# A convolution over pairs of tiles with its taps on ScalarE, weight sums kept in HBM, and 18 of 44 down groups by seven products instead of 12

## The chip, the core and the metric

The kernel runs on one core of a Trainium2 chip. The metric is the time of one execution on the device in microseconds; lower is better. Before the change the median of three timed runs is 1498.99 us.

## What is computed

One transformer block on 256 tokens of width 2048, batch 1. A mixer (forgetting attention, stick-breaking attention, attention over 256 memory tokens, gated and summed, projected by `w_out`) is followed by a feed-forward part. The change concerns the feed-forward part only:

```python
h2 = rms_norm(x, g_ffn[l])
u = causal_depthwise_conv(h2 @ w_up[l], conv_w[l], conv_b[l])   # 3 taps per channel
u_gate, u_val = jnp.split(u, 2, axis=-1)                        # 5632 channels each
x = x + (jax.nn.silu(u_gate) * u_val) @ w_down[l]               # 5632 -> 2048
```

All inputs are float32, and the output is compared in float32 precision.

## The kernel before, in words

**Precision.** Every weight is split into two float32r parts: `hi`, a rounded copy made by ScalarE, and `lo`, the rest, made by VectorE as `raw - hi`. Activations are held as hi and lo halves side by side (256 + 256 columns). A product takes three matmuls (hi by hi, lo by hi, hi by lo), or, in the up stage, one matmul of 512 columns (`hi` weights against hi and lo activations at once, L739) and one of 256 columns (`lo` weights against hi activations, L740).

**Weights.** `piece` (up stage, L130 to L141) and `load` with `parts` (down stage, L783 to L794) bring 512 KB of weights per step. SyncE (SP) issues the DMA into one of four `raw` buffers, ScalarE casts it into one of four `hi` buffers (L136, L792), VectorE makes the `lo` (L137, L793). SP has one queue in program order, so a load whose buffer isn't free holds up the loads behind it. A `raw` buffer is free when `lo` is made, a `hi` or `lo` buffer when TensorE has used it.

**Up stage** (L729 to L745). Eleven steps `f0` over four channel tiles of 128; for each, `s = 0` (gate) and `s = 1` (value): 22 rounds. A round accumulates four tiles in four PSUM banks over eight pieces of two rows of tiles (`k`), 64 pairs of matmuls of L739 and L740. After the round each of the four tiles is handed to `conv` (L705), whose instructions are issued while the next round's matmuls run: ScalarE copies the lo half out of PSUM (L710), VectorE adds the hi half and multiplies by the row scale (L712, L713), ScalarE does the third tap with the bias (L716), VectorE the two others (L717, L718). In a value round follow the product with the gate (L724) and the split into `aT` (L169, L170).

**Down stage** (L865 to L894). The 44 channel tiles are 22 pairs, and the 2048 output columns are two halves `nb`: 44 groups of two tiles by 1024 columns, each a 2 by 2 by 2 block product. `eight` does a group as eight products of 128 by 512, 24 matmuls. `seven` does it as seven products (21 matmuls) in the Strassen-Winograd form: three products add straight into the outputs X, four go into extra sums Y, and `gather` (L846) adds up Y at the end of the half. The seven products need sums of the activations (`forms`, L767) and sums of the weights (t13 and t24, L828, L829, L832, L833), made by VectorE right in the group from the freshly loaded weights. The order of groups is a string: `plans = ("eeee" + "see" * 5 + "eee", "eee" + "se" * 7 + "eeeee")`, so 5 + 7 = 12 groups are done by seven products.

**What sets the order.** TensorE, ScalarE, VectorE, GpSimd and SP each run one queue in order; a scheduler places the instructions of each queue by priority when the program is built. `later` and `tick` say after which piece a `conv`, `gather` or the like is issued. A program's eight PSUM banks are handed out one at a time by `bank`.

## Time and profile before

| | |
|---|---|
| median of three timed runs (lowest to highest) | 1498.99 us (1498.02 to 1499.24) |
| span of the profiled execution, first to last instruction | 1494.4 us |
| TensorE / its weight loads busy | 99% / 84% of the span |
| VectorE / ScalarE / GpSimd busy | 68% / 53% / 1% |
| granted TensorE clock | full in every slice |
| DMA | 283.62 MB, mean 190 GB/s |
| up stage, first to last matmul | 766.0 to 1255.2 us |
| down stage, last matmul begins | 1489.7 us |

The page has no time of its own for the profiled execution beside its span; the median lies 4.6 us above the span, which is what lies around the first and the last instruction. In the rows of the profile, PE is TensorE, PEld its weight loads, DVE VectorE, ACT ScalarE, POOL GpSimd, and SP SyncE; `L137` is a line of the kernel. A row of a group gives the operation with its output and input, the count, then the time in all, the mean of one in ns, and the idle time ahead of it with what ended it.

### The profile page before, as it was taken

To read this page: it belongs to the slowest core of one execution; us is meant where nothing else is said; L and a number is where in the kernel's file an instruction comes from. 1 tells how busy PE (TensorE), PEld (TensorE's weight loads), DVE (VectorE), ACT (ScalarE), POOL (GpSimd) and SP (SyncE) were. 2 spreads that over 40 slices of the span, in tenths; PEclk is the share of its full clock that TensorE was granted. 3 is DMA by queue.
4 is the path that set the end of the run, shared out by engine and by line. 5 is a ranking of instruction groups with operands and counts; after the bars stand their busy time and mean duration, and the time that the engine had idled before them with its cause. 6 is when DMAs were issued, how large, how long until landed. Compare 5 with 4: busy or idle time off the path is not lost.

```text
span 1494.4 us, 19871 instructions
## 1 busy us (share of the span) xinstructions
PE 1483.2 (99%) x7429; PEld 1255.9 (84%) x7429; DVE 1014.0 (68%) x1465; ACT 794.0 (53%) x1108; POOL 16.1 (1%) x46
## 2 busy tenths in 40 slices
PE   8999999999999999999999999999999999999998
PEld 6888888888888888888888888888888888888777
DVE  5767566555655646555557778777778778987885
ACT  6755454358544444444456556556556656553552
POOL 0000000001000000000000000000000000000000
PEclk9999999999999999999999999999999999999999
DMA  8665475365666666655555665655656565556554
GB/s 291 193 211 158 126 220 167 119 211 164 188 194 210 185 210 203 185 190 190 184 182 183 198 191 184 196 190 184 198 187 191 186 196 183 199 188 228 185 202 140
DMA packets 138543, 283.62 MB, mean 190 GB/s; under 512 B 9275, under 2 KB 18127, under 8 KB 138447
## 3 DMA queue, kind: packets, MB, share of 16 engines
q1 hardware_dynamic: 137118, 280.26, 59.0%
q10 hardware_dynamic: 1328, 2.11, 0.4%
q8 instruction: 58, 0.95, 0.2%
q14 instruction: 39, 0.31, 0.1%
HBM read 280.23 MB, written 2.10 MB: 189 GB/s over the span
## 4 chain that ended last, share of the span: by engine, by line
PE 95%; DMA 2%; ACT 1%; DVE 1%; issue 0%; POOL 0%; SPq 0%; DVEq 0%; POOLq 0%; ACTq 0%
PE u L739 21%; PE u L740 11%; PE g L147 5%; PE g L148 5%; PE g L149 5%; PE x L797 4%; PE x L798 4%; PE x L799 4%; PE s L147 2%; PE s L149 2%; PE f L147 2%; PE f L149 2%; PE s L148 2%; PE f L148 2%; PE o L147 2%; PE o L149 2%
## 5 line engine op out<-in xcount | busy, mean ns | idle before, releaser
L739 PE MATMUL u<-hT,hi_u 128*128 128x512 f32 x1408 | 488.5, 392 | 0.0
L740 PE MATMUL u<-hT,lo_u 128*128 128x256 f32 x1408 | 395.1, 281 | 0.0
L739 PEld LDWEIGHTS u<-hT,hi_u 128*128 128x128 f32 x1408 | 263.3, 187 | 57.3
L137 DVE TENSOR_TENSOR lo_u<-raw_u,hi_u 128x1024 fp32r<-128x1024 f32 x176 | 215.4, 1224 | 116.0 <-ACT hi_u L136 115.9
L740 PEld LDWEIGHTS u<-hT,lo_u 128*128 128x128 f32 x1408 | 266.8, 189 | 0.0
L136 ACT CAST hi_u<-raw_u 128x1024 fp32r<-128x1024 f32 x176 | 184.7, 1050 | 138.4 <-PE u L739 106.5
L137 DVE TENSOR_TENSOR lo_g<-raw_g,hi_g 128x1024 fp32r<-128x1024 f32 x96 | 117.7, 1229 | 101.3 <-ACT hi_g L136 98.8
L136 ACT CAST hi_g<-raw_g 128x1024 fp32r<-128x1024 f32 x96 | 100.7, 1051 | 121.8 <-PE g L148 97.4
L147 PE MATMUL g<-hi_g,xT 128*128 128x512 f32 x384 | 151.1, 393 | 0.0
L149 PE MATMUL g<-lo_g,xT 128*128 128x512 f32 x384 | 149.8, 390 | 0.0
L148 PE MATMUL g<-hi_g,xT 128*128 128x512 f32 x384 | 149.7, 390 | 0.0
L792 ACT CAST hi_d<-raw_d 128x1024 fp32r<-128x1024 f32 (+1 forms) x88 | 86.7, 993 | 74.6 <-PE x L798 38.7
L793 DVE TENSOR_TENSOR lo_d<-raw_d,hi_d 128x1024 fp32r<-128x1024 f32 (+1 forms) x88 | 99.8, 1148 | 16.2 <-ACT hi_d L792 16.2
L797 PE MATMUL x<-hi_d,aT 128*128 128x512 f32 x268 | 104.4, 390 | 0.0
L799 PE MATMUL x<-lo_d,aT 128*128 128x512 f32 x268 | 104.4, 390 | 0.0
L798 PE MATMUL x<-hi_d,aT 128*128 128x512 f32 x268 | 104.4, 390 | 0.0
L149 PEld LDWEIGHTS g<-lo_g,xT 128*128 128x128 f32 x384 | 72.1, 188 | 15.2
L148 PEld LDWEIGHTS g<-hi_g,xT 128*128 128x128 f32 x384 | 72.2, 188 | 14.5
L147 PEld LDWEIGHTS g<-hi_g,xT 128*128 128x128 f32 x384 | 72.2, 188 | 14.6
L137 DVE TENSOR_TENSOR lo_s<-raw_s,hi_s 128x1024 fp32r<-128x1024 f32 (+1 forms) x40 | 44.7, 1118 | 37.2 <-ACT hi_s L136 37.2
L137 DVE TENSOR_TENSOR lo_f<-raw_f,hi_f 128x1024 fp32r<-128x1024 f32 (+1 forms) x40 | 44.7, 1120 | 34.5 <-ACT hi_f L136 33.0
L136 ACT CAST hi_f<-raw_f 128x1024 fp32r<-128x1024 f32 (+1 forms) x40 | 38.5, 966 | 52.5 <-PE f L148 47.6
(318 smaller groups left out, 2554.3 us busy)
## 6 DMA issues: line engine op xcount, KB each, us to landing
raw_u<-in_w_up_dram SPq DMA_DIRECT2D x176, 512.0 KB, 4.0
raw_g<-in_w_in_dram SPq DMA_DIRECT2D x96, 512.0 KB, 3.6
raw_d<-in_w_down_dram SPq DMA_DIRECT2D x88, 512.0 KB, 4.7
raw_f<-in_w_in_dram SPq DMA_DIRECT2D x32, 512.0 KB, 3.5
raw_s<-in_w_in_dram SPq DMA_DIRECT2D x32, 512.0 KB, 3.4
raw_o<-in_w_out_dram SPq DMA_DIRECT2D x32, 512.0 KB, 4.7
raw_kv<-in_w_mem_kv_dram SPq DMA_DIRECT2D x15, 512.0 KB, 5.4
raw_b<-in_w_br_fox_dram SPq DMA_DIRECT2D x12, 512.0 KB, 4.0
```

The lines of the kernel that those rows point to most:

```text
L136: pin(nc.scalar.copy(hi[:, :m], raw[:, :m]))
L137: pin(nc.vector.tensor_tensor(lo[:, :m], raw[:, :m], hi[:, :m].bitcast(F32), ALU.subtract))
L147: nc.tensor.matmul(o, lhsT=xh, rhs=wh, start=first, stop=False)
L148: nc.tensor.matmul(o, lhsT=xl, rhs=wh, start=False, stop=False)
L149: nc.tensor.matmul(o, lhsT=xh, rhs=wl, start=False, stop=last)
L739: nc.tensor.matmul(ps[i], lhsT=hi[:, j, c], rhs=hT[:, k + j, :], start=first, stop=False)
L740: nc.tensor.matmul(ps[i][:, :S], lhsT=lo[:, j, c], rhs=hT[:, k + j, :S], start=False, stop=last)
L792: nc.scalar.copy(hi[:, :n], src)
L793: nc.vector.tensor_tensor(lo[:, :n], src, hi[:, :n].bitcast(F32), ALU.subtract)
L797: nc.tensor.matmul(o, lhsT=ah, rhs=w[0], start=first, stop=False)
L798: nc.tensor.matmul(o, lhsT=al, rhs=w[0], start=False, stop=False)
L799: nc.tensor.matmul(o, lhsT=ah, rhs=w[1], start=False, stop=last)
```

## The change

**Convolution.** `conv` now takes a pair of tiles whose sums lie in two neighbouring PSUM banks, allocated together (`two_banks`, a pool of four pairs in place of eight single banks from the up stage on). Each instruction of 256 columns per tile becomes one of 512 per pair, except where a tap's factor differs by tile. The first and second taps, one fused multiply-add on VectorE each, become a multiplication on ScalarE (L738, one per tile and tap) into a scratch tile and an addition on VectorE (L739, one per pair and tap). The scaled sums `u` of all pairs share one buffer; there were two.

**Weight sums.** The four sums of a group's weights that `seven` needs are made in the up stage by `weight_sums`, one group in each of the first 18 rounds: SP loads the group's two weight tiles (2 x 512 KB) into `r`, VectorE makes the four sums in place, GpSimd's queue writes the 1 MB to a tensor T in HBM. In the down stage `seven` loads the sums (2 x 512 KB, `load_sums`) and the weights (256 KB + 512 KB, since one quarter isn't needed by itself), and VectorE only splits them.

**Plans.** `PLANS = ("eee" + "se" * 8 + "eee", "eee" + "se" * 4 + "sse" * 3 + "ee")`: 8 + 10 = 18 groups by seven products, so 26 by eight.

**Memory.** `aT` is split in two (36 and 8 tiles) so that `r` has room during the first 36; forms 8 and 9 go into the slots of tiles that are used up. The first up matmul waits for a pair of banks.

The diff, cut to its core:

```diff
+NSEVEN = (8, 10)
+PLANS = ("eee" + "se" * 8 + "eee", "eee" + "se" * 4 + "sse" * 3 + "ee")
...
     def bank(name):
+        if pp2:
+            return pp2[0].tile([P, 2, 512], F32, tag="pair", name=name)[:, 0]
         return pp.tile([P, 512], F32, tag="bank", name=name)
...
+    ppx.close()
+    pp2.append(ctx.enter_context(tc.tile_pool(name="pp2", bufs=4, space=bass.MemoryType.PSUM, reuse_waits="tile")))
...
+    def scratch(name):
+        return sm.tile([P, 512], F32, tag="junk", bufs=2, name=name).rearrange("p (i s) -> p i s", i=2)
+
+    def conv(ps, f, s):
+        taps_of = lambda j, i: taps[:, j, s * FT + f + i : s * FT + f + i + 1]
+        cr = scratch(f"cr_{f}_{s}")
+        nc.scalar.copy(cr, ps[:, :, S:])
+        nc.vector.tensor_tensor(cr, cr, ps[:, :, :S], ALU.add)
+        nc.vector.tensor_tensor(u[:, :, 2:], cr, rbc.unsqueeze(1).to_broadcast([P, 2, S]), ALU.mult)
+        y = cp.tile([P, 2, S], F32, tag="y", name=f"y_{f}_{s}")
         for i in range(2):
...
-        nc.scalar.activation(y, u[:, 2:], AF.Identity, scale=tap(2), bias=tap(3))
-        nc.vector.scalar_tensor_tensor(y, u[:, 1 : S + 1], tap(1), y, ALU.mult, ALU.add)
-        nc.vector.scalar_tensor_tensor(y, u[:, 0:S], tap(0), y, ALU.mult, ALU.add)
+            nc.scalar.activation(y[:, i], u[:, i, 2:], AF.Identity, scale=taps_of(2, i), bias=taps_of(3, i))
+        for j in (1, 0):
+            z = scratch(f"z{j}_{f}_{s}")
+            for i in range(2):
+                nc.scalar.activation(z[:, i], u[:, i, j : j + S], AF.Copy, scale=taps_of(j, i))
+            nc.vector.tensor_tensor(y, y, z, ALU.add)
...
+    def weight_sums(nb, p):
+        n0 = nb * PIECE
+        r = sp.tile([P, 2, 2, 512], F32, tag="r", name=f"r_{nb}_{p}")
+        for j in range(2):
+            tc.keep_in_program_order(
+                nc.sync.dma_start(r[:, j].rearrange("p a n -> p (a n)"), dv[:, 2 * p + j, n0 : n0 + PIECE])
+            )
+        yield
+        b01 = r[:, 0, 1]
+        tc.keep_in_program_order(nc.vector.tensor_tensor(r[:, 0, 0], r[:, 0, 0], b01, ALU.add))
+        tc.keep_in_program_order(nc.vector.tensor_tensor(b01, b01, r[:, 1, 1], ALU.add))
+        yield
+        tc.keep_in_program_order(nc.vector.tensor_tensor(r[:, 1, 1], r[:, 1, 1], r[:, 0, 0], ALU.add))
+        tc.keep_in_program_order(nc.vector.tensor_tensor(r[:, 1, 0], r[:, 1, 0], r[:, 1, 1], ALU.add))
+        T = dram.tile([P, 2, 1024], F32, name=f"T_{nb}_{p}")
+        nc.gpsimd.dma_start(T, r.rearrange("p a b n -> p a (b n)"))
+        made[nb, p] = T
+        yield
...
+                if k in (2, 8, 12):
+                    for a in adding:
+                        next(a)
                 tick()
-            for i in range(4):
-                later(conv(ps[i], f0 + i, s))
+            for i in (0, 2):
+                later(conv(pairs[i // 2], f0 + i, s))
...
+    def load_sums(T, h, name):
+        t = down_pool().tile([P, PIECE], F32, tag="tt", name=f"tt{h}_{name}")
+        nc.sync.dma_start(t, T[:, h])
+        return t
...
     def seven(p, n0, X, Y, first, last):
         k0, k1 = 2 * p, 2 * p + 1
-        raw0, raw1 = load(k0, n0), load(k1, n0)
-        t13 = sums(f"t13_{n0}_{p}")
-        t24 = sums(f"t24_{n0}_{p}")
-        b01, b11 = raw0[:, 512:], raw1[:, 512:]
-        nc.vector.tensor_tensor(t13[:, :512], raw0[:, :512], b01, ALU.add)
-        nc.vector.tensor_tensor(t13[:, 512:], b11, b01, ALU.add)
-        (B00,) = parts(raw0[:, :512], f"d{n0}_{k0}")
+        T = made[n0 // PIECE, p]
+        raw0, raw1 = load(k0, n0, 512), load(k1, n0)
+        t13, t42 = (load_sums(T, h, f"{n0}_{p}") for h in range(2))
+        (B00,) = parts(raw0, f"d{n0}_{k0}")
         three(Y[0], *a_of(k0, 0), B00, first, last)
-        nc.vector.tensor_tensor(t24[:, :512], t13[:, :512], b11, ALU.add)
-        nc.vector.tensor_tensor(t24[:, 512:], t24[:, :512], raw1[:, :512], ALU.add)
         B10, B11 = parts(raw1, f"d{n0}_{k1}")
...
-    plans = ("eeee" + "see" * 5 + "eee", "eee" + "se" * 7 + "eeeee")
```

Three places show how the change moves instructions in the queues of the engines. In the rows the number at a name's end is only a buffer's, `[waits ...]` names what the instruction waits for.

TensorE at the step from the output projection (`o3`) to the up stage, before. `u0_0` to `u3_0` are the four tiles of the first round, each in a bank of its own:

```order
L148 MATMUL o3_1_6034<-hi_o3_14_6184,mT_3_1_5627 128x512
L149 MATMUL o3_1_6034<-lo_o3_14_6185,mT_3_1_5627 128x512
L739 MATMUL u0_0_6213<-hT_5522,hi_u0_0_0_6218 128x512 [waits Activation_49]
L740 MATMUL u0_0_6213<-hT_5522,lo_u0_0_0_6219 128x256 [waits DVE_49]
L739 MATMUL u1_0_6214<-hT_5522,hi_u0_0_0_6218 128x512 [waits PE_49]
L740 MATMUL u1_0_6214<-hT_5522,lo_u0_0_0_6219 128x256
L739 MATMUL u2_0_6215<-hT_5522,hi_u0_0_0_6218 128x512
```

The same place in the changed kernel, where `u0_0` holds tiles 0 and 1:

```order
L155 MATMUL o3_1_6034<-hi_o3_14_6184,mT_3_1_5627 128x512
L156 MATMUL o3_1_6034<-lo_o3_14_6185,mT_3_1_5627 128x512
L791 MATMUL u0_0_6224<-hT_5522,hi_u0_0_0_6227 128x512 [waits DVE_49,Activation_49]
L792 MATMUL u0_0_6224<-hT_5522,lo_u0_0_0_6228 128x256
L791 MATMUL u0_0_6224<-hT_5522,hi_u0_0_0_6227 128x512
L792 MATMUL u0_0_6224<-hT_5522,lo_u0_0_0_6228 128x256
```

The first up matmul used to wait for its weights (ScalarE) and now waits for VectorE as well. The matmuls with the `lo` weights behind it have lost their own wait for VectorE, so the value waited for lies beyond those weights' `lo`; the next instructions of VectorE that read PSUM banks there are the two additions of `o3` to the residual.

VectorE in the up stage, while round `f0 = 12, s = 0` runs and the values of tiles 8 to 11 are convolved, before. `cr`, `y` and `u` are the convolution's, `lo_u12_0_10` is the `lo` of the round's sixth piece:

```order
L712 TENSOR_TENSOR cr_10_1_7601<-cr_10_1_7601,u10_1_7317 128x256 [waits Activation_49]
L170 TENSOR_TENSOR aT_6209<-y_8_0_7345,aT_6209 128x256 [waits Activation_49]
L170 TENSOR_TENSOR aT_6209<-y_9_0_7354,aT_6209 128x256 [waits Activation_49]
L713 TENSOR_TENSOR u_0_6457<-cr_10_1_7601,rbc_5524 128x256 [waits DVE_49]
L712 TENSOR_TENSOR cr_11_1_7612<-cr_11_1_7612,u11_1_7318 128x256
L137 TENSOR_TENSOR lo_u12_0_8_7669<-raw_u12_0_8_7667,hi_u12_0_8_7668 128x1024 [waits DMAHW3_49,PE_49]
L717 SCALAR_TENSOR_TENSOR y_10_1_7605<-u_0_6457,taps_108,y_10_1_7605 128x256 [waits Activation_49]
L713 TENSOR_TENSOR u_1_6459<-cr_11_1_7612,rbc_5524 128x256 [waits DVE_49]
L718 SCALAR_TENSOR_TENSOR y_10_1_7605<-u_0_6457,taps_108,y_10_1_7605 128x256 [waits DVE_49]
L137 TENSOR_TENSOR lo_u12_0_10_7691<-raw_u12_0_10_7689,hi_u12_0_10_7690 128x1024 [waits DMAHW4_49,PE_49]
```

The same place in the changed kernel; `z1`, `z0` are the products made by ScalarE, `r_0_6` the weight sums:

```order
L739 TENSOR_TENSOR y_8_1_7580<-y_8_1_7580,z1_8_1_7583 128x512 [waits Activation_49]
L739 TENSOR_TENSOR y_8_1_7580<-y_8_1_7580,z0_8_1_7587 128x512 [waits DVE_49,Activation_49]
L730 TENSOR_TENSOR cr_10_1_7594<-cr_10_1_7594,u10_1_7334 128x512 [waits Activation_49]
L745 TENSOR_TENSOR y_8_0_7361<-y_8_0_7361,y_8_1_7580 128x512 [waits DVE_49]
L731 TENSOR_TENSOR u_6222<-cr_10_1_7594,rbc_5524 128x2x256 [waits DVE_49]
L144 TENSOR_TENSOR lo_u12_0_8_7683<-raw_u12_0_8_7681,hi_u12_0_8_7682 128x1024 [waits DMAHW1_49,PE_49,Activation_49]
L748 TENSOR_TENSOR aT0_6213<-y_8_0_7361,aT0_6213 128x2x256 [waits Activation_49]
L764 TENSOR_TENSOR r_0_6_7634<-r_0_6_7634 128x512 [waits DMAHW5_49,DMASW4_49]
L739 TENSOR_TENSOR y_10_1_7598<-y_10_1_7598,z1_10_1_7601 128x512 [waits Activation_49]
L765 TENSOR_TENSOR r_0_6_7634<-r_0_6_7634 128x512 [waits DMAHW6_49,DVE_49]
L739 TENSOR_TENSOR y_10_1_7598<-y_10_1_7598,z0_10_1_7605 128x512 [waits DVE_49,Activation_49]
L144 TENSOR_TENSOR lo_u12_0_10_7707<-raw_u12_0_10_7705,hi_u12_0_10_7706 128x1024 [waits DMAHW2_49,PE_49]
```

VectorE now goes from the first pair's last tap (`z0`) straight to the second pair's chain, and, the `lo` apart, waits four times for ScalarE ahead of `lo_u12_0_10`, with two of the four weight sums between.

VectorE in the second half of the down stage, around the second group by seven products, before. `t13` and `t24` are the sums, `lo_t13`, `lo_t24` their splits:

```order
L793 TENSOR_TENSOR lo_t13_1024_0_12192<-t13_1024_0_12168,hi_t13_1024_0_12191 128x1024 [waits PE_49,Activation_49]
L828 TENSOR_TENSOR t13_1024_1_12251<-raw_d1024_2_12247 128x512 [waits DMAHW1_49,DVE_49]
L829 TENSOR_TENSOR t13_1024_1_12251<-raw_d1024_3_12249,raw_d1024_2_12247 128x512 [waits DMAHW2_49]
L793 TENSOR_TENSOR lo_t24_1024_0_12202<-t24_1024_0_12169,hi_t24_1024_0_12201 128x1024 [waits PE_49,Activation_49]
L793 TENSOR_TENSOR lo_d1024_20_12214<-raw_d1024_20_12211,hi_d1024_20_12213 128x1024 [waits DMAHW7_49,PE_49,Activation_49]
```

The same place in the changed kernel, where the split sums come from the loaded `tt0`, `tt1`:

```order
L853 TENSOR_TENSOR lo_d1024_2_12272<-raw_d1024_2_12263,hi_d1024_2_12271 128x512 [waits DMAHW7_49,PE_49,Activation_49]
L853 TENSOR_TENSOR lo_d1024_3_12279<-raw_d1024_3_12265,hi_d1024_3_12278 128x1024 [waits DMAHW0_49,PE_49,Activation_49]
L853 TENSOR_TENSOR lo_t13_1024_1_12289<-tt0_1024_1_12267,hi_t13_1024_1_12288 128x1024 [waits DMAHW1_49,PE_49,Activation_49]
L836 TENSOR_TENSOR aT1_10208<-fr_8_12255,aT1_10208 128x4x128 [waits PE_49,Activation_49]
L831 TENSOR_TENSOR fr_9_12345<-fd_9_12344 128x256 [waits DVE_49]
L853 TENSOR_TENSOR lo_t42_1024_1_12299<-tt1_1024_1_12269,hi_t42_1024_1_12298 128x1024 [waits DMAHW2_49,Activation_49]
L853 TENSOR_TENSOR lo_d1024_34_12311<-raw_d1024_34_12308,hi_d1024_34_12310 128x1024 [waits DMAHW3_49,PE_49,Activation_49]
```

Before, the sums of the next group (L828, L829, which wait for its weights' DMA) stood between the splits `lo_t13` and `lo_t24` of the group in work. Now the splits wait for the loaded sums, and only a form of the activations (L836, L831) stands between.

150 lines of the change are left out of this document (86 added, 64 removed).

## The prediction

> **What bounds the kernel now.** I read the page's busy times first, then its chain of work that ended last, then the table of windows over the up stage and the stretches of the down stage.
>
> ```profile
> PE 1483.2 (99%) x7429; PEld 1255.9 (84%) x7429; DVE 1014.0 (68%) x1465; ACT 794.0 (53%) x1108; POOL 16.1 (1%) x46
> PE 95%; DMA 2%; ACT 1%; DVE 1%; issue 0%; POOL 0%; SPq 0%; DVEq 0%; POOLq 0%; ACTq 0%
> 766.00:1166.00 400.00, 400.00 (x2312) 353.07 (x2311) 298.77 (x493) 237.09 (x362) 0.00 (x0) 1.00 0.60 190
> 1255.00:1300.00 45.00, 45.00 (x201) 37.30 (x200) 42.72 (x72) 25.99 (x34) 0.00 (x0) 1.00 0.55 180
> 1300.00:1375.00 75.00, 75.00 (x332) 62.16 (x331) 62.31 (x87) 37.12 (x40) 0.00 (x0) 1.00 0.63 209
> 1375.00:1440.00 65.00, 62.85 (x273) 50.71 (x273) 51.56 (x60) 32.91 (x35) 0.00 (x0) 1.00 0.59 195
> 1440.00:1490.00 50.00, 50.00 (x221) 41.12 (x219) 33.69 (x37) 20.32 (x21) 0.00 (x0) 1.00 0.49 168
> ```
>
> In the windows the columns are the stretch, its length, then busy time and count of PE, PEld, DVE, ACT and POOL, the granted clock, the DMA share and GB/s. TensorE is busy 99% and carries 95% of the chain, so time changes where it has fewer matmuls, or where it is made to wait. A down matmul of 512 columns takes 50.00 / 221 = 0.2262 us in the last window. By that pace 1255 to 1300 and 1300 to 1375 are full (201 and 332 matmuls, 45.5 and 75.1 us), and 1375 to 1440 holds 65.00 - 273 x 0.2262 = 3.2 us without matmuls: the only stall of the two stages. Three rows of the timeline show its largest piece.
>
> ```profile
> 1391.53 0.69 DVE L829 TENSOR_TENSOR t<-raw_d,raw_d 128x512 f32<-128x512 f32 x1 [1.44 <-DMA raw_d<-in_w_down_dram]
> 1392.13 1.22 DVE L793 TENSOR_TENSOR lo_t<-t,hi_t 128x1024 fp32r<-128x1024 f32 x1
> 1393.41 0.50 PE L799 MATMUL y<-lo_t,sf 128*128 128x512 f32 x1 [1.43 <-DVE lo_t L793]
> ```
>
> VectorE, in order, stood 1.44 us at the next group's sum (L829), whose weights had not landed; `lo_t` of the group in work queued behind it, and TensorE waited 1.43 us for `lo_t`.
>
> The up stage has no stall. What keeps it so is how early the splits are made, from the tile's groups and its waits:
>
> ```profile
> L739 PE MATMUL u<-hT,hi_u x1408: 389/391/476, 766.0 to 1255.0; 128*128 128x512 f32 x176
> L137 DVE TENSOR_TENSOR lo_u<-raw_u,hi_u 128x1024 fp32r<-128x1024 f32 x176 | 215.4, 1224 | 116.0 <-ACT hi_u L136 115.9
>   ACT hi_u L136: 106.5, 93
> ```
>
> 489 us for 22 rounds is 22.2 us a round, 2.78 us a piece, 0.347 us a pair of matmuls. The third row is under those who waited for L739: the cast waits for a buffer that TensorE frees. With four buffers a cast starts three pieces (8.3 us) ahead of its use, so a `lo` is ready about 8.3 - 1.05 - 1.22 = 6 us early. The convolution eats into that in the rounds that carry it.
>
> **The change part by part.** *Matmuls.* 12 groups of 21 and 32 of 24 are 1020 matmuls; 18 and 26 are 1002. 18 x 0.2262 = **-4.1 us**, if TensorE stays fed.
>
> *The stalls at 1375 to 1440.* L828 and L829 no longer exist in the down stage; `lo_t` waits for a loaded sum that is asked for well ahead. **-3.2 us**, between 0 (the wait for the load takes their place) and -3.2. Late next would be that load, counted below.
>
> *Start of the up stage.*
>
> ```profile
> 765.50 1.41 DVE L685 TENSOR_TENSOR xres<-xres,o 128x512 f32<-128x512 f32 x2
> ```
>
> The first up matmul began at 766.0 (row above). It now waits for VectorE; the last two readers of the old banks are these additions, which end at 765.50 + 1.41 = 766.91. **+0.9 us**; bounds 0 (only the first addition counts) and 0.9. Behind it nothing queues but matmuls; VectorE and ScalarE only get further ahead.
>
> *Convolution.* Its price is paid on ScalarE and VectorE beside TensorE. The rows, per tile before, and the nearest ones for 512 columns and for a scaled copy:
>
> ```profile
> L710 ACT COPY cr<-u 128x256 f32<-128x256 f32 x88 | 29.4, 365 | 16.9 <-PE u L740 16.9
> L712 DVE TENSOR_TENSOR cr<-cr,u 128x256 f32<-128x256 f32 x88 | 34.1, 418 | 0.0
> L713 DVE TENSOR_TENSOR u<-cr,rbc 128x256 f32<-128x256 f32 x88 | 34.2, 420 | 0.0
> L716 ACT ACTIVATE y<-u,taps 128x256 f32<-128x256 f32 x88 | 49.2, 595 | 14.7 <-DVE u L713 14.7
> L717 DVE SCALAR_TENSOR_TENSOR y<-u,taps,y 128x256 f32<-128x256 f32 x88 | 39.5, 479 | 0.1
> L718 DVE SCALAR_TENSOR_TENSOR y<-u,taps,y 128x256 f32<-128x256 f32 x88 | 39.6, 480 | 0.1
> L724 DVE TENSOR_TENSOR y<-y,y 128x256 f32<-128x256 f32 x44 | 17.5, 420 | 0.0
> L170 DVE TENSOR_TENSOR aT<-y,aT 128x256 fp32r<-128x256 f32 x44 | 17.6, 422 | 4.7 <-ACT aT L169 4.7
> L169 ACT CAST aT<-y 128x256 fp32r<-128x256 f32 x44 | 17.1, 407 | 24.3 <-DVE y L724 24.3
> L172 ACT ACTIVATE hT<-hT,gmix_c 128x256 fp32r<-128x256 f32 x16 | 6.8, 470 | 3.8 <-DVE hT L174 3.8
> L169 ACT CAST mT<-mt 128x256 fp32r<-128x256 f32 x16 | 5.9, 370 | 10.8 <-DVE mT L170 10.8
> L136 ACT CAST hi_s<-raw_s 128x512 fp32r<-128x512 f32 x8 | 5.0, 620 | 10.6 <-PE s L148 10.6
> L685 DVE TENSOR_TENSOR xres<-xres,o 128x512 f32<-128x512 f32 x8 | 5.5, 684 | 0.1
> L136 ACT CAST hi_u<-raw_u 128x1024 fp32r<-128x1024 f32 x176 | 184.7, 1050 | 138.4 <-PE u L739 106.5 <-issue 16.4 <-PE o L148 6.6
> ```
>
> A round in which values are convolved is the heavier one. VectorE before: 8 `lo` of 1.22 and four tiles of 0.418 + 0.420 + 0.479 + 0.480 + 0.420 + 0.422 = 2.64, 20.3 us. After: 8 x 1.22, twelve additions and products of 512 columns at 0.69 (0.684, L685), and four weight sums at 0.69: 20.8 of 22.2 us (a round with gates: 9.8 + 8 x 0.69 + 4 x 0.69 = 18.0). ScalarE before: 8 x 1.05 + 4 x (0.365 + 0.595 + 0.407) = 13.9. The multiplication on ScalarE is not in the trace. I estimate it as a plain cast and what a factor adds, 0.407 + (0.470 - 0.370) = 0.51, between 0.41 (L169) and 0.595 (L716). A pair then costs 0.62 + 2 x 0.595 + 4 x 0.51 + 0.62 = 4.5, and the round 8.4 + 9.0 = 17.4 us. Both fit, so throughput costs nothing.
>
> The order is tighter. Of the rows shown of VectorE's queue, `lo_u12_0_10` (sixth piece) stands behind the second pair's `z0`. From the first pair's last matmul, 0.5 us before the round's end: copy 0.62, two VectorE steps 1.38, six ScalarE steps 1.19 + 2.04, copy 0.62, then two casts of `hi` 2.1 and the cast of `aT` 0.62 (which stand ahead of the second pair's taps, and cover three VectorE steps), six ScalarE steps 3.23, addition 0.69, `lo` 1.22: 13.7, so done 13.2 us into the round. TensorE wants it at 5 x 2.78 + 0.23 = 14.1. Cover left: 0.9 us, where it was about 6. I take **0**: back-to-back pairs of such steps overlap a little, and the middle estimate leaves cover; with 0.41 or 0.595 for eight products it would be 1.7 or 0.2.
>
> *Weight sums.* Each of 18 rounds reads 1.05 MB and writes 1.05 MB more: 2.1 MB in 22.2 us, 94 GB/s on top of 190. The stretch moved 190 GB/s at a share of 0.60, so full would be about 317; 284 is 90%. SP issues two more loads per round:
>
> ```profile
> L135 SPq DMA_DIRECT2D raw_u<-in_w_up_dram x176: 367/368/742, 748.4 to 1235.6; - x176
> DMA to landing us min/median/max: 3.3/4.0/4.6
>   DVE t L828: 12.2, 9
> DMA to landing us min/median/max: 3.5/4.7/6.4
> ```
>
> 0.37 us each beside eight of 22.2 us. The load for `r` stands in SP's queue and waits until the write two rounds ago has left that slot; that is 22 us old, and `raw_u` behind it has some 5 us. GpSimd's queue is empty there (x0 in the windows), so the write waits for nobody. VectorE's wait for `r` comes a third of a round after its issue, against the 4.0 us of `raw_u`. Cost taken: **0**, bounds 0 and the rival on DMA below; a gain is excluded, since nothing is removed.
>
> *Down loads.* A seven now loads 1.84 MB in 21 x 0.226 = 4.75 us of TensorE, an eight 1.05 MB in 5.43 us. `se` is 2.88 MB in 10.2 us, 283 GB/s; `sse` 4.72 MB in 14.9 us, 316 GB/s, against 191 at 0.57, 335 in full. Only where two sevens adjoin (three times) is a load late by position. The second's `t42` goes into the slot of the first's, which is free when that one's `hi` and `lo` are made (1.05 + 1.22), by my reading of the order about 2.3 us after the first seven's first matmul. TensorE wants the second's `lo` after 36 matmuls and two more, at 8.14 + 0.45 = 8.6 us, so it has to land 2.27 earlier, at 6.3. That leaves 4.0 us for a landing of 3.5, 4.7 or 6.4 (last row, of `raw_d`; the row of 12.2 us is of the waits that go). That is 0, 0.7 or 2.4 us each; three times 0 to 7.2. I take **+1.0**: near the shortest, because the queue ahead of it is then empty. VectorE per seven falls, since 4 sums of 0.69 go.
>
> The tail (`gather`, additions, the output) keeps its work and lies behind the same last eights.
>
> Sum against the median, with the 4.6 us around the span unchanged: 1498.99 - 4.1 - 3.2 + 0.9 + 1.0 = **1493.6 us**. The bounds of the terms give 1498.99 - 7.3 = 1491.7 and 1498.99 - 4.1 + 0 + 0.9 + 7.2 = 1503.0.
>
> **Rivals.** 0.2% is 3.0 us, about what a measurement of this kernel tells from no change: 1496.0 and 1502.0 are the borders.
>
> *Taps on ScalarE arrive late (slower).* If the chain above is longer than its cover of 0.9 us, TensorE waits at `lo` of the sixth piece in each of 10 rounds with values. From 0.55 us over it eats the gain; at 1 us over the time is 1493.6 + 10 = 1503.6. For: ten handovers between engines that I have counted at nothing, and waits on one buffer `u`. Against: TensorE's delay gives every later piece the same time back, and L716 and L710 run beside each other's ends. 0.20: 0.04 within, 0.16 slower. The Trainium skill speaks against the change here: "ScalarE: Activation LUTs", under "Rules for kernel authors", would have multiplications on VectorE and not on ScalarE. By row the fused tap on VectorE was 0.48 and its replacement is 0.51 on ScalarE plus 0.34 on VectorE, so the trace agrees that work is added; whether it shows is a matter of the cover.
>
> *The down stage trades matmuls for loads.* If each of 18 sevens waits 0.3 us for its loads, the time is 1499.0, at 0.5 us slower. For: 94% of the DMA rate in `sse`. Against: 0.49 to 0.63 now, and eights between. 0.12: 0.07 within, 0.05 slower.
>
> *The old stalls stay under a new name.* `lo_t` waits for `tt` as it did for L829: 1493.6 + 3.2 = 1496.8. Against: VectorE no longer stands at the next group's data first. 0.06, within.
>
> *The up stage fills the DMA.* If a write costs twice its share, the 18 rounds need 1.05 of what there is: 0.05 x 400 = 20 us, 1513. Against: writes were nearly absent, so nothing shows such a price. The Trainium skill ("DMA: Bandwidth & Descriptors", "Issuing engines are not separate DMA queues") says that GpSimd's writes run on the same 16 engines as SP's loads; no row here shows it, since GpSimd moved little. 0.04, slower.
>
> That fewer matmuls are not issued is excluded by the plans.
>
> **How the numbers follow.** Forecast 0.58 (its own range 1491.7 to 1497: 0.55 faster, 0.03 within). Faster 0.55; within 0.03 + 0.04 + 0.07 + 0.06 = 0.20; slower 0.16 + 0.05 + 0.04 = 0.25. The range 1491.5 to 1503.0 takes the forecast, the second and third rivals and the milder half of the first, some 8 in 10.
>
> **What would show it.** Right: 1002 matmuls in the down stage at 0.226 us; no gap in its middle; a first up matmul held to about 766.9 by L692 (the old L685); ScalarE about 78% and VectorE about 87% busy (20.8 and 18.0 us in turn) in the up stage, DMA share about 0.9, matmuls still 0.347 us a pair. Wrong: waits of TensorE for `lo_u` at the sixth piece once every second round (first rival); for `lo_t` in many sevens (second) or only where the gaps were (third); `raw_u` landing in far more than 4.0 us (fourth).

## The result and the profile after

The changed kernel takes 1517.31 us (median of four executions, 1515.66 to 1523.52), the kernel before 1499.12: 1.0131 times as long, 95% interval 1.011 to 1.0151. The forecast was 1493.6 us, in a range up to 1503.0. The profiled execution took 1516.09 us with a span of 1514.4, so 1.7 us lie around the span here.

The page of the changed kernel: busy times, groups of the up stage, and DMA issues with the us to landing.

```profile
span 1514.4 us, 20053 instructions
PE 1492.3 (99%) x7411; PEld 1254.3 (83%) x7411; DVE 1021.5 (67%) x1291; ACT 856.8 (57%) x1211; POOL 25.8 (2%) x64
L792 PE MATMUL u<-hT,lo_u 128*128 128x256 f32 x1408 | 396.0, 281 | 7.6 <-DVE lo_u L144 7.6
L143 ACT CAST hi_u<-raw_u 128x1024 fp32r<-128x1024 f32 x176 | 181.8, 1048 | 144.0 <-DMA raw_u<-in_w_up_dram 87.6
raw_u<-in_w_up_dram SPq DMA_DIRECT2D x176, 512.0 KB, 4.7
r<-in_w_down_dram SPq DMA_DIRECT2D x36, 512.0 KB, 7.3
T<-r POOLq DMA_DIRECT2D x18, 1024.0 KB, 7.7
```

TensorE has 18 matmuls fewer and is busy 9 us longer. Two things are new: ScalarE's casts wait 87.6 us for weights (`raw_u`), and TensorE waits for `lo_u`. The second row of each pair of up matmuls, from the views of that tile of after and of before, bounds the stage:

```profile
L792 PE MATMUL u<-hT,lo_u x1408: 274/280/389, 764.9 to 1270.5; 128*128 128x256 f32 x176
```
```profile
L740 PE MATMUL u<-hT,lo_u x1408: 277/281/285, 766.2 to 1255.2; 128*128 128x256 f32 x176
```

With the first up matmul at 764.6 (766.0 before) the stage is 505.9 us, where it was 489.2: +16.7. The down stage from the first to the last matmul is 1270.6 to 1508.2, 237.6 us, where it was 234.3: +3.3. From the last matmul to the end of the span it is 6.2 us, where it was 4.7: +1.4. The up stage begins 1.5 us earlier, at code that is unchanged; over all runs below that moment lies between 764.1 and 765.9. Together that is the difference of the spans, 20.0 us, up to rounding. I take the parts in this order.

**Up stage, one value round.** The timeline of ScalarE in the round that began at 901.5 us, then of VectorE and TensorE at the fifth and sixth piece:

```profile
904.20 1.05 ACT L143 CAST hi_u<-raw_u 128x1024 fp32r<-128x1024 f32 x1 [5.89 <-DMA raw_u<-in_w_up_dram]
905.16 0.58 ACT L729 COPY cr<-u 128x512 f32<-128x512 f32 x1
907.87 1.10 ACT L734 ACTIVATE y<-u,taps 128x256 f32<-128x256 f32 x2 [1.18 <-DVE u L731]
908.87 1.69 ACT L738 ACTIVATE z<-u,taps 128x256 f32<-128x256 f32 x4
```
```profile
915.40 0.69 DVE L739 TENSOR_TENSOR y<-y,z 128x512 f32<-128x512 f32 x1
916.01 0.68 DVE L765 TENSOR_TENSOR r<-r 128x512 f32<-128x512 f32 x1
916.62 0.68 DVE L739 TENSOR_TENSOR y<-y,z 128x512 f32<-128x512 f32 x1
917.22 1.22 DVE L144 TENSOR_TENSOR lo_u<-raw_u,hi_u 128x1024 fp32r<-128x1024 f32 x1
914.28 0.38 PE L792 MATMUL u<-hT,lo_u 128*128 128x256 f32 x1 [1.11 <-DVE lo_u L144]
918.49 0.39 PE L792 MATMUL u<-hT,lo_u 128*128 128x256 f32 x1 [1.16 <-DVE lo_u L144]
```

ScalarE stands 5.89 us at a cast whose weights have not landed. The first step of the convolution (L729) stands behind it in ScalarE's queue: it starts at 905.16, though its sums are ready at about 901. The chain that the prediction timed then runs as predicted, but four microseconds late, and TensorE waits for `lo` of the fifth and of the sixth piece. Why the weights are late shows in the windows (stretch, length, busy time and count of PE, PEld, DVE, ACT, POOL, granted clock, DMA share, GB/s), and in the DMA's issues from 893 to 905 us; the last two rows are the same window of before:

```profile
878.00:893.00 15.00, 15.00 (x87) 12.99 (x86) 11.21 (x15) 11.80 (x21) 0.00 (x0) 1.00 0.80 285
893.00:905.00 12.00, 12.00 (x70) 10.40 (x69) 5.72 (x6) 4.29 (x5) 0.53 (x1) 1.00 0.97 355
905.00:920.00 15.00, 12.73 (x71) 10.60 (x70) 13.74 (x18) 12.79 (x23) 0.00 (x0) 1.00 0.47 138
raw_u<-in_w_up_dram SPq DMA_DIRECT2D x4, 512.0 KB, 8.2
T<-r POOLq DMA_DIRECT2D x1, 1024.0 KB, 7.7
```
```profile
893.00:905.00 12.00, 12.00 (x71) 10.62 (x70) 8.55 (x15) 6.95 (x12) 0.00 (x0) 1.00 0.61 196
raw_u<-in_w_up_dram SPq DMA_DIRECT2D x4, 512.0 KB, 3.5
```

The average is what I worked out, but it comes in bursts: the next group's loads of `r` (issued at 891.5), the write of the last sums (896.7) and four loads of `raw_u` fall together, the DMA is at 0.97, and `raw_u` takes 8.2 us to land instead of 3.5 in the same window of before. Afterwards the DMA idles at 0.47.

**Up stage, the rounds between.** Five rounds with stalls (with `f0` = 8, 12, 20, 28, 32, `s` = 0) are 11.5 us longer than 22.19 in all. But twelve others, with no wait at all, are 22.62 us each, 0.43 longer. From the starts of the matmuls, a pair takes 0.353 us in them instead of 0.347. A window of after past the last stall, and one of before:

```profile
1160.00:1260.00 100.00, 100.00 (x568) 86.76 (x567) 75.82 (x88) 73.91 (x116) 0.53 (x1) 1.00 0.68 211
```
```profile
1140.00:1240.00 100.00, 100.00 (x579) 88.23 (x578) 76.69 (x130) 60.06 (x95) 0.00 (x0) 1.00 0.60 189
```

568 matmuls in 100 us against 579, at full granted clock. The first rounds of after, with all the added traffic, run at 22.19; the slow beat begins with the first stall, ends with the one of `f0` = 28 and begins again with the one of `f0` = 32, and it goes on through four rounds without any weight sums.

**Down stage.** By the pace of 0.2266 us, the 1001 steps between the starts of 1002 matmuls are 226.8 us; 10.8 us are lost. The first seven loses 6.3 of them. Timelines of SP, ScalarE and TensorE there, then a window:

```profile
1260.08 25.61 SPq L840 DMA_DIRECT2D raw_d<-in_w_down_dram  x10
1285.74 10.74 SPq L845 DMA_DIRECT2D tt<-T  x4
1292.10 1.04 ACT L852 CAST hi_t<-tt 128x1024 fp32r<-128x1024 f32 x1 [4.04 <-DMA tt<-T]
1293.20 0.53 PE L857 MATMUL d<-hi_t,sf 128*128 128x512 f32 x1 [3.63 <-ACT hi_t L852]
1293.00:1297.00 4.00, 3.50 (x8) 2.37 (x9) 3.82 (x4) 4.00 (x6) 0.00 (x0) 0.57 0.32 102
```

The sums' first load is issued at 1285.74, behind ten loads of `raw_d`, the last of them for groups that come later. The cast of these sums starts at 1292.10, when TensorE has stood for 2.5 us, and TensorE goes on at 1293.20, after 3.6 us. The matmuls behind that stop start 0.43 us apart, twice the usual, and the granted clock is 0.57 in that window. The Trainium skill ("TensorE: Matmul & The Clock Gate", "HAM oscillation — how this bites in real kernels") warns of gaps over about 3.4 us for that reason; this trace agrees, at 3.6, but other runs show that the length of one gap does not decide alone (last section). The other 4.4 us are lost from 1455 us on, at the three places where two sevens adjoin:

```profile
ACT hi_t L852 <- DMA tt<-T: 8.4, 5, 3.4
PE d L859 <- DVE lo_t L853: 1.2, 3, 0.5
PE d L857 <- ACT hi_t L852: 1.2, 2, 0.6
```

By the count of matmuls, TensorE stops at the second group's `t42` in the first of these places, and at its `t13` in the two others.

**The end.** The first two of the last additions, in after and in before:

```profile
1505.95 1.28 DVE L954 TENSOR_TENSOR o<-xres,d 128x512 f32<-128x512 f32 x2 [2.36 <-PE d L859]
```
```profile
1486.00 0.69 DVE L893 TENSOR_TENSOR o<-xres,x 128x512 f32<-128x512 f32 x1 [4.72 <-PE x L799]
1487.37 0.69 DVE L893 TENSOR_TENSOR o<-xres,x 128x512 f32<-128x512 f32 x1 [0.67 <-PE x L799]
```

Before, the first addition began 3.7 us ahead of the last matmul (1489.66), the second 1.4 us behind the first. Now both banks of a pair are handed over together, 2.3 us ahead of the last matmul (1508.24). The difference is the 1.4 us at the end; the cause is read from these rows and was not tried apart. In every run below with pairs of banks the span ends 6.1 to 6.4 us behind the last matmul, in the two with single banks 4.9 us.

### The profile page after: what moved, and what is told of

Read it like the earlier page. It is cut to its first block, busy times and chain, and to the rows that moved or that the text cites. A ratio compares the mean times of both kernels' runs of the same rounds, so it can differ in the third digit from the quotient of the medians.

```text
span 1514.4 us, 20053 instructions
## 1 busy us (share of the span) xinstructions
PE 1492.3 (99%) x7411; PEld 1254.3 (83%) x7411; DVE 1021.5 (67%) x1291; ACT 856.8 (57%) x1211; POOL 25.8 (2%) x64
## 4 chain that ended last, share of the span: by engine, by line
PE 74%; DMA 9%; DVE 9%; ACT 5%; issue 3%; POOL 0%; SPq 0%; DVEq 0%; ACTq 0%; POOLq 0%
PE u L791 9%; DMA raw_u<-in_w_up_dram 7%; PE g L154 5%; PE g L156 5%; PE g L155 5%; PE u L792 5%; PE d L859 4%; PE d L858 4%; PE d L857 4%; DVE lo_u L144 3%; PE s L154 2%; PE s L156 2%; PE f L154 2%; PE s L155 2%; PE f L155 2%
## 5 line engine op out<-in xcount | busy, mean ns | idle before, releaser
L791 PE MATMUL u<-hT,hi_u 128*128 128x512 f32 x1408 | 495.7, 397 | 0.1
L143 ACT CAST hi_u<-raw_u 128x1024 fp32r<-128x1024 f32 x176 | 181.8, 1048 | 144.0 <-DMA raw_u<-in_w_up_dram 87.6
L852 ACT CAST hi_d<-raw_d 128x1024 fp32r<-128x1024 f32 (+1 forms) x88 | 83.6, 963 | 42.5 <-PE d L858 29.6
L853 DVE TENSOR_TENSOR lo_d<-raw_d,hi_d 128x1024 fp32r<-128x1024 f32 (+1 forms) x88 | 95.1, 1110 | 15.0 <-ACT hi_d L852 15.0
L857 PE MATMUL d<-hi_d,aT 128*128 128x512 f32 x246 | 95.7, 389 | 0.0
L858 PE MATMUL d<-hi_d,aT 128*128 128x512 f32 x246 | 95.7, 389 | 0.0
L859 PE MATMUL d<-lo_d,aT 128*128 128x512 f32 x246 | 95.7, 389 | 0.0
L738 ACT ACTIVATE z<-u,taps 128x256 f32<-128x256 f32 x176 | 74.6, 496 | 0.0
L739 DVE TENSOR_TENSOR y<-y,z 128x512 f32<-128x512 f32 x88 | 60.7, 690 | 19.1 <-ACT z L738 16.3
L853 DVE TENSOR_TENSOR lo_t<-tt,hi_t 128x1024 fp32r<-128x1024 f32 x36 | 44.1, 1225 | 39.8 <-ACT hi_t L852 39.7
```

What stands on the lines that cost most here:

```text
L143: pin(nc.scalar.copy(hi[:, :m], raw[:, :m]))
L791: nc.tensor.matmul(ps, lhsT=hi[:, j, c], rhs=hT[:, k + j, :], start=first, stop=False)
L852: nc.scalar.copy(hi[:, :n], src)
L853: nc.vector.tensor_tensor(lo[:, :n], src, hi[:, :n].bitcast(F32), ALU.subtract)
L857: nc.tensor.matmul(o, lhsT=ah, rhs=w[0], start=first, stop=False)
L858: nc.tensor.matmul(o, lhsT=al, rhs=w[0], start=False, stop=False)
```

## The experiments

The theory after the result: **bursts** of DMA in the up stage make weights late, and two places of the down stage ask too late for the sums. The rivals: the convolution's chain with taps on ScalarE is too long by itself; the four additions on VectorE use up the cover; the traffic is too much in any order.

**e1_no_sums**: the changed kernel without its weight sums; the down stage reads `w_down` in place of them.

```diff
-            adding = [weight_sums(*asked.pop(0))] if asked and f0 < HEAD else []
+            adding = []
...
-        T = made[n0 // PIECE, p]
+        T = dv[:, 2 * p : 2 * p + 2, n0 : n0 + PIECE]
```

> Leaves out the weight sums: the down stage reads rows of w_down of the same size in their place, so its output is not the reference's. Traffic theory (the sums' loads and writes crowd the weights of the up stage, ScalarE stands at a late cast, the convolution starts late): the up stage falls from 505.9 to 489-490 us, every round 22.2 us, no wait of TensorE for lo_u; the time falls by 15-17 us to about 1501. Chain theory (six scaled copies a pair on ScalarE are too long by themselves): the rounds with values still stall by 1 to 3 us each, up stage 500 or more.

Measured: up stage 764.4 to 1253.7, 489.3 us, every round after the first 22.19; no wait for `lo_u`. The profiled execution took 1500.44 us, the median of ten is 1502.03 (three of them above 1509, see e9_clean_start). In the profiled execution the whole +16.7 goes with the weight sums. The rival on the taps does not fall by this run alone: without the sums VectorE's queue has another order, in which `lo_u` of the sixth piece stands ahead of the second pair's taps and not behind them as in the changed kernel. It is ready 4.4 us before its use, as in the kernel before (4.4). e6 below keeps the changed kernel's order.

**e2_fused_taps**: the changed kernel with the two taps on VectorE.

```diff
-            z = scratch(f"z{j}_{f}_{s}")
             for i in range(2):
-                nc.scalar.activation(z[:, i], u[:, i, j : j + S], AF.Copy, scale=taps_of(j, i))
-            nc.vector.tensor_tensor(y, y, z, ALU.add)
+                nc.vector.scalar_tensor_tensor(
+                    y[:, i], u[:, i, j : j + S], taps_of(j, i), y[:, i], ALU.mult, ALU.add
+                )
```

> Only the two taps go back to VectorE, fused as before (four instructions of 256 columns per pair at 0.48 us each in place of four scaled copies on ScalarE and two additions). Chain theory: no stall, up stage 489-490 us. Traffic theory: the weights still land late (up to 9 us, ScalarE still waits 80 us or so for them), but the chain behind a late start is 2 us a pair shorter, so TensorE's stalls shrink from 11 us to 0-5 and the up stage is 489-496 us. Neither: 505 us as now.

Measured: 1511.44 us (1508.19 to 1513.51), up stage 502.3 us, TensorE waits 4.7 us for `lo_u` instead of 7.6; ScalarE still waits 89.8 us for `raw_u`. The stalls shrank within what the burst theory gave, but the stage is 6 us above its range; 4.3 of them are the slow beat, which I had left out and which stayed in ten rounds that have no stall.

**e3_loads_later**: other places in the round for loads, additions and write.

```diff
-                if k in (2, 8, 12):
+                if k in (8, 12, 14):
```

> The same work; only the weight sums' loads, first and second additions are issued later in the round (after pieces 8, 12, 14 instead of 2, 8, 12 of 16 rows), so that a round's loads no longer fall on the write of the sums of the round before. Traffic theory: the waits of ScalarE for raw_u fall from 88 us to under 40, up stage 490-498 us, time about 1505. Chain theory: the chain is the same, up stage about 505 us.

Measured: 1517.42 us (1514.64 to 1522.63), up stage 508.0. A miss, and a mistake in the making: the write moved along with the loads. In the round at 994.1 us the write is issued at 993.58, between the two loads of `r` at 993.13 and 993.64, and ScalarE stands as before:

```profile
1006.39 1.05 ACT L143 CAST hi_u<-raw_u 128x1024 fp32r<-128x1024 f32 x1 [5.23 <-DMA raw_u<-in_w_up_dram]
```

What it does tell: in this kernel's order `lo_u` of the sixth piece stands ahead of the second pair's taps, not behind them, with no weight sums between them and the fifth piece's, and TensorE waits for it all the same. Late weights suffice.

**e4_plans**: other plans of the down stage, 15 sevens.

```diff
-NSEVEN = (8, 10)
-PLANS = ("eee" + "se" * 8 + "eee", "eee" + "se" * 4 + "sse" * 3 + "ee")
+NSEVEN = (8, 7)
+PLANS = ("eeee" + "se" * 8 + "ee", "eee" + "se" * 7 + "eeeee")
```

> Only the order of groups: the first seven comes one eight later, and the second half has 7 sevens with an eight between each (15 in all, so 1011 down matmuls instead of 1002). If the stalls of the down stage come from where the sums' loads stand (behind the end of the convolution for the first seven, behind the neighbour's buffers where two sevens adjoin): 1011 x 0.2266 = 229.1 us plus under 1.5 us of stall, against 226.8 + 10.8 now, so 7 us faster. If loads of the sums are late in general (rate of the DMA): each of 15 sevens still waits 0.3 us or more, 234 us or above. The up stage has 3 rounds of sums fewer, which lie without stalls behind the 15 kept: its time stays within 3 us of 505.9.

Measured: 1505.93 us (1503.98 to 1508.19), ratio to before 1.0051, interval 1.0036 to 1.0066. The down stage is 1268.4 to 1499.7, 231.3 us with nine matmuls more, 2.4 us of it lost. That is above the 1.5 expected, but TensorE stops for a split at two places and not in each of 15 sevens, as a lack of rate would have had it (234 or above): place, not rate. The up stage is 503.5.

The next three start from e4_plans. **e5_apart** takes a group's loads and the write of the group before it apart by half a round:

```diff
-            adding = [weight_sums(*asked.pop(0))] if asked and f0 < HEAD else []
+            adding = [weight_sums(*asked.pop(0))] if f0 + s == 0 else coming
+            coming = [weight_sums(*asked.pop(0))] if asked and f0 < HEAD else []
...
-                if k in (2, 8, 12):
+                if k in ((2, 8, 12) if f0 + s == 0 else (0, 2)):
                     for a in adding:
                         next(a)
+                if k == 14:
+                    for a in coming:
+                        next(a)
```

> The plans of e4_plans, and the weight sums spread over two rounds: the loads are issued after the last piece of a round, the additions and the write early in the next, so that by the earlier trace's offsets a load starts about 11 us after the write of the group before and not together with it. Burst theory (the average traffic fits, the coincidence of loads and write does not): ScalarE waits for raw_u under 30 us in all, TensorE for lo_u under 1 us, up stage 489-491 us against 503.5, time 1491-1494. Rate theory (284 of 317 GB/s is too much in any order): waits and stalls stay, up stage 498 or more.

Measured: 1494.97 us (median of eight; six from 1493.86 to 1495.23, two at 1502.17 and 1503.51), ratio to before 0.9989, interval 0.9969 to 1.0008. In the profiled execution every round after the first is 22.19 and the stage 489.6; the tile's row, a window over the rounds with sums, and ScalarE's waits at the casts:

```profile
L793 PE MATMUL u<-hT,lo_u x1408: 277/280/284, 765.4 to 1254.7; 128*128 128x256 f32 x176
778.00:1105.00 327.00, 326.83 (x1887) 287.95 (x1886) 272.61 (x326) 232.11 (x356) 8.12 (x15) 1.00 0.84 280
ACT hi_u L143 <- PE u L792: 96.7, 71, 2.3
```

280 GB/s at a share of 0.84, more on average than in the changed kernel (268 in the same window), and ScalarE's casts wait for nothing but free buffers again (third row). So the average fits, and the rate theory falls. The landings of `raw_u` show what did change, in the changed kernel, in e3 and in e5:

```profile
DMA to landing us min/median/max: 3.5/4.7/9.1
DMA to landing us min/median/max: 3.4/4.7/12.1
DMA to landing us min/median/max: 3.5/4.7/6.6
```

The median is the same, the late ones are gone. Against the changed kernel this run moves `lo_u` of the sixth piece, too, ahead of the second pair's taps and of the additions, so by itself it does not acquit these. But e3 has the same order of VectorE there, with loads and write together, and stalls; the two differ in the place of the transfers (and in 18 groups against 15).

**e6_no_write** leaves out the write of the sums, and **e7_no_adds** the additions.

```diff
-        nc.gpsimd.dma_start(T, r.rearrange("p a b n -> p a (b n)"))
```

> e4_plans without the write of the sums to HBM; the down stage reads rows of w_down of the same size, so the output is not the reference's. Loads of r and additions stay. Both traffic theories: 237 GB/s is light, up stage 489-490 us, no stall. Additions theory (four more instructions in VectorE's queue, waiting for r, use up the cover): stalls at the sixth piece stay, up stage 495 or more.

```diff
-        tc.keep_in_program_order(nc.vector.tensor_tensor(r[:, 0, 0], r[:, 0, 0], b01, ALU.add))
...
-        tc.keep_in_program_order(nc.vector.tensor_tensor(r[:, 1, 0], r[:, 1, 0], r[:, 1, 1], ALU.add))
```

> e4_plans without the four additions per group: r is loaded and written unchanged, so the output is not the reference's. Traffic theories: the weights land late as now, ScalarE waits 60 us or more for raw_u, up stage 496-504. Additions theory: no stall, 489-490.

In e6 as in e1 the down stage reads rows of `w_down` in place of the sums. Measured: e6 1494.34 us (1493.52 to 1496.63; ratio 0.9971, interval 0.9962 to 0.9981), up stage 490.0; e7 1493.38 (seven of ten from 1492.45 to 1494.57, three from 1501.49 to 1502.62), up stage 489.3. In e6 the additions stand between the second pair's taps as in the changed kernel, and the `lo` of the sixth piece is ready 1.2 to 1.9 us ahead of its use in the value rounds from `f0` = 8 to 20: the chain that I had priced at a cover of 0.9 us holds, when weights come less late (ScalarE still waits 32.0 us for `raw_u` here, against 87.6). In e1 and e5 that cover is 4.4 us, so in e6 the order and the remaining waits take some 3 us of it without a stall; in the changed kernel, with the same order, later weights take the rest. So neither the chain nor the additions stall TensorE by themselves. Against the expectation e7 has no stall either. Without additions its write waits for the loads alone and comes earlier, and ScalarE waits 6.2 us for `raw_u` in all; so e7 took the burst apart as well and decides nothing between the theories.

**e8_one_stall**: the kernel before with one long instruction on VectorE.

```diff
+                if (f0, s, k) == (12, 1, 8):
+                    w = aT[:, 28:42].rearrange("p f (l q) -> p (f l) q", l=2)
+                    b = rbc.unsqueeze(1).to_broadcast([P, 28, S])
+                    tc.keep_in_program_order(nc.vector.tensor_tensor(w, b, b, ALU.mult))
```

> The kernel before with one extra instruction on VectorE (7168 columns, about 7.5 us) ahead of lo_u of the fifth piece of the eighth round (f0 = 12, s = 1); it writes into a part of aT that is overwritten later. Theory that a stall leaves TensorE in a slower beat: one stall of 2 to 3 us, then pairs at 0.350 us instead of 0.347, rounds of 22.6 us instead of 22.2 until another stall or the stage's end, up stage +8 to +9 us in all. Rival (the slower beat has to do with the added traffic or the new layout): +2 to +3 us, and pairs at 0.347 after it.

Measured: 1507.47 us, ratio 1.0058 (1.0043 to 1.0073); up stage 500.5 us, +11.3. Windows ahead of the stall, behind its stop, and later:

```profile
820.00:920.00 100.00, 100.00 (x579) 88.19 (x578) 74.68 (x122) 57.13 (x87) 0.00 (x0) 1.00 0.65 193
936.00:941.00 5.00, 4.75 (x20) 4.24 (x21) 3.60 (x4) 1.00 (x1) 0.00 (x0) 0.66 0.73 218
950.00:1050.00 100.00, 100.00 (x568) 86.67 (x568) 77.04 (x132) 58.50 (x91) 0.00 (x0) 1.00 0.62 183
```

One stop of about 3.7 us, some 1.7 of lowered clock, then 14 rounds of 22.62: 14 x 0.43 = 6.0. This is the kernel before, without the added traffic, so an interruption alone can start the slow beat.

**e9_clean_start**: e5_apart without sums in the first round.

```diff
-            adding = [weight_sums(*asked.pop(0))] if f0 + s == 0 else coming
+            adding = [] if f0 + s == 0 else coming
...
-                if k in ((2, 8, 12) if f0 + s == 0 else (0, 2)):
+                if k in (0, 2):
```

> e5_apart with no weight sums in the first round (the 15 groups go into rounds two to sixteen). Some executions of e5_apart are 8 to 9 us longer than the rest. If those are executions in which the slow beat starts in the first round (21 rounds x 0.43 = 9.0 us), where the additions hold up VectorE ahead of rb, for which TensorE waits: none of them here, all executions 1493-1496 us, clearly faster than before by 3 to 5 us. If the long executions come from elsewhere, about a quarter of them stay at 1502-1504.

Measured: 1502.88 us; eight of twelve executions from 1501.73 to 1503.70, four from 1493.73 to 1495.03; ratio 1.0003 (0.9986 to 1.0019). The profiled one, of 1501.73, has no wait for `lo_u`, but the slow beat from the first round on, 498.5 us:

```profile
L793 PE MATMUL u<-hT,lo_u x1408: 277/281/286, 764.7 to 1262.8; 128*128 128x256 f32 x176
```

The size is as expected (21 x 0.43 = 9.0), the cause that I named is not: with the additions out of the first round the slow beat came more often (e5 and e9 ran on different chips, so the chip is not excluded as a reason). That round is interrupted by eight transposes in any kernel, and in all fourteen traces with alternating matmuls, from before to e12, the beat changes there. In e9 to e12 the pairs take 0.347 ahead of the transposes and 0.353 behind; in e5, and in the kernel before, it is the other way round. So the beat of the long rest goes with the beat in which the stage's first two pieces ran, and what sets that one is open. The two groups of e1, e5 and e7 lie as far apart; that they are the same two beats was only argued, since no profile fell on a long one.

**e10_fused_clean**, **e11_first_seven** and **e12_sixteen** change one thing each in e9_clean_start: the taps as in e2; `PLANS[0]` back to `"eee" + "se" * 8 + "eee"`; an eighth seven in the second half (`"eee" + "se" * 8 + "eee"`).

> e9_clean_start with the two taps fused on VectorE again. If the place of the taps only matters where weights land late: the same time within 1 us and an up stage of 489-490 us in both. If the taps on ScalarE were needed to make room on VectorE for the sums: stalls for lo_u return, 495 or more.

> e9_clean_start with the first seven one eight earlier, where the change had it (three eights ahead instead of four). If that place alone makes the 4 us stop and the slowed matmuls behind it (the loads of the sums stand on SP's queue behind the end of the convolution): down stage 4 to 7 us longer, one wait of TensorE for hi_t of 3 us or more. If the long stop came of the late up stage (the convolution ending late): down stage the same within 1 us.

> e9_clean_start with an eighth seven in the second half (16 in all), still with an eight between each two. Three matmuls fewer are 0.7 us; if no load of sums is late in that place, the time is 0.7 us shorter than e9_clean_start, if one is, the same or up to 2 us longer.

Measured: e10 1502.20 us (nine of ten from 1501.83 to 1503.06), within 0.7 of e9, no stall, up stage 498.5 in both: the place of the taps does not matter where the weights come in time. e11 1507.51; its down stage is 235.6 us against 230.3 in e9, with one wait again:

```profile
PE d L861 <- ACT hi_t L856: 3.5, 1, 3.5
```

So the place of the first seven costs 5.3 us by itself, after an up stage that ends without stalls. e12 1501.77: 1.1 us under e9, with ten of eleven executions in the longer group. Its down stage is 230.1 us against 230.3, so of the 0.7 us that three matmuls are worth the traces show 0.3; the rest is within the spread of the runs.

**e13_by_two** and **e14_by_four**: e9_clean_start with the up matmuls grouped by 2 and by 4; **e15_stall_by_two**: e8_one_stall grouped by 2.

```diff
-                    for i in range(4):
...
-                        nc.tensor.matmul(ps, lhsT=hi[:, j, c], rhs=hT[:, k + j, :], start=first, stop=False)
-                        nc.tensor.matmul(ps[:, :S], lhsT=lo[:, j, c], rhs=hT[:, k + j, :S], start=False, stop=last)
+                    for i0 in range(0, 4, 2):
+                        for i in range(i0, i0 + 2):
...
+                            nc.tensor.matmul(ps, lhsT=hi[:, j, c], rhs=hT[:, k + j, :], start=first, stop=False)
+                        for i in range(i0, i0 + 2):
...
+                            nc.tensor.matmul(ps[:, :S], lhsT=lo[:, j, c], rhs=hT[:, k + j, :S], start=False, stop=last)
```

> e9_clean_start with the up matmuls in the order hi, hi, lo, lo over two tiles instead of hi, lo, hi, lo. If the slow beat (0.353 us a pair, 9 us over the stage) belongs to the strict alternation of 512 and 256 columns, it does not appear, and all executions are near 1494 us. If two short matmuls in a row cannot hide their weight loads (0.19 us each beside 0.117), every pair is longer, up to 0.376, and the stage up to 40 us longer. If the beat belongs to neither, two thirds of the executions stay at 1502-1504.

> The same with four hi and then four lo. As for by_two: near 1494 in all executions, or longer where the short matmuls wait for their weight loads, more so than by two.

> e8_one_stall (the kernel before with one long stall in the eighth round) with the matmuls in the order hi, hi, lo, lo. If the alternation carries the slow beat, the rounds after the stall are as long as the rounds ahead of it; if not, they are 0.4 us longer each, as in e8_one_stall.

Measured: e13 1496.41 us, all eleven executions from 1495.03 to 1498.04, ratio to before 0.9988 (0.9979 to 0.9997); every round after the first 22.29. e14 1499.26 (1497.54 to 1500.05), rounds of 22.45, ratio 1.0002. e15 1505.51; the windows as in e8:

```profile
820.00:920.00 100.00, 100.00 (x575) 87.22 (x574) 73.80 (x123) 56.85 (x87) 0.00 (x0) 1.00 0.66 193
950.00:1050.00 100.00, 100.00 (x577) 87.25 (x576) 77.80 (x134) 58.28 (x90) 0.00 (x0) 1.00 0.64 187
```

575 and 577 matmuls ahead of and behind the stall: no slow beat, and the up stage is 495.0 us, as 489.2 + 21 x 0.10 + the stop of 3.7. In e13 and e15 the beat is the same on both sides of the eight transposes, too, where every alternating trace changes it. The second beat belongs to the strict alternation of 512 and 256 columns; two by two costs 0.10 us a round and shows one beat only. (e13 to e15 ran on another chip than e1 to e12, whose three chips all show both beats.) Of the versions that do the whole work, e13 is the one that is faster than both kernels by its interval, by 0.1% against before.

## Why the prediction was wrong, point by point

- **Matmuls, -4.1: right.** 1002 in the down stage at 0.2266 us where nothing is late.
- **Old stalls, -3.2: right that they go**, and with L828 and L829 they did. What comes late next was mis-sized, two points down.
- **Start of the up stage, +0.9:** right in kind, 0.3 in size: the first up matmul starts 0.54 us after the one ahead of it, where the pace is 0.23. It starts 0.15 us behind the first of the two additions and ahead of the second's end, which is the case that I gave as the lower bound.
- **Down loads, +1.0: 10.8.** Adjoining sevens cost 4.4, inside the bounds 0 to 7.2, of which I took the low end. The sentence "Only where two sevens adjoin (three times) is a load late by position" failed: the first seven has one too, since SP's queue puts its sums behind weights of later groups, and 6.3 us went there, some of it because the stop was long enough to lower the clock. I had counted the convolution's end as a matter of the up stage only.
- **Convolution, 0: right** where weights come in time: by e6 in the changed kernel's order, by e1 and e10 in others. A scaled copy took 0.496 us (estimated 0.51), and its chain was sized well enough (cover 0.9 forecast, 1.2 to 1.9 in e6).
- **Weight sums, 0: the step that failed.** I set the mean, 284 of 317 GB/s, against the rate in full, and the landing of 4.0 us measured at a share of 0.60. Loads and write fall together, the share is 0.97 for 12 us, landings double, and ScalarE in order passes the lateness to the convolution, whose cover is thin at that point. e5 moves the same bytes a round, with loads and write apart, and loses nothing.
- **The end, 0: +1.4**, for an addition that now waits for both banks of a pair.
- **The time around the span:** I added 4.6 us, the median less the span. It is 1.7 us for the execution profiled here; the one of before was some 3 us shorter than the median.
- **The rivals.** The first (0.20) had the place, the rounds with values at the sixth piece, and nearly the price (1 us in ten rounds forecast, about 2 us in five measured) right, and the cause wrong. The fourth (0.04) had the cause, DMA in the up stage, with a wrong reason (a write at twice its share) and nearly the right sum, 1513. They are one mechanism, which the prediction priced in two places: the chain's cover of 0.9 us for weights that come in time, the traffic with some 5 us to spare for `raw_u`, as if no convolution stood behind a late cast. The second (0.12) asked for a wait in each of 18 sevens; the waits are at four of them. The third (0.06) did not happen.
- **In no step:** the slow beat, 5 of the 16.7 us.

What stays open: which of the two beats an interruption leaves behind, and in which one the stage begins. The eight transposes change the beat in every alternating trace; of the later stops some start the slow beat, some end it, and some leave it as it is.

## What to carry to other kernels

Added transfers are to be placed on a time axis together with the transfers that they may meet: a share that fits on average says nothing while loads and a write of 1 MB each are issued within about 5 us. Where an engine takes its work in order, a late input of one stream delays the other streams behind it, so the cover of a chain and the lateness of the loads ahead of it belong in one sum. A load for the first group of a stage wants its place in the queue checked, not only its buffer.

## What the runs showed of the hardware

- The alternating stream of 512 and 256 columns has two beats, 0.347 and 0.353 us a pair, at full granted clock. In the fourteen alternating traces every change of beat lies at an interruption, or in one case (e2, at 1123.9 us) 2.8 us behind one. In the order hi, hi, lo, lo a pair takes 0.348 in both traces (22.29 us for 64 pairs).
- A load of 512 KB lands in 3.5 us at a DMA share of 0.61 and in 8.2 us at 0.97.
- After stops of TensorE of 3.5 to 3.7 us (e8, e11, e1, after, e3) the matmuls ran at about half pace, for some 3 us (granted clock 0.57 in after and 0.66 in e8, in windows of 4 and 5 us) and in e1 for some 7 us (0.54 from 1276 to 1283 us). Single stops of up to 1.2 us in the changed kernel's up stage were not followed by it. The length of one stop does not decide alone: after 3.35 us in e15 the clock stayed at 1.00 (937 to 941 us), after 2.9 us in e2 it was 0.52 (1288 to 1295 us), and in e3 two stops of 1.0 and 1.9 us with 0.5 us of work between them were followed by 0.59 (1150 to 1154 us).
